# A decoder layer on one core: low parts on GpSimd in halves, output weights split sooner, key pages in groups of four

## The chip, the core and the metric

The kernel runs on one core of a Trainium2 chip. The metric is the device time of one execution in microseconds (us); the median of three runs of the kernel before is 780.32 us (780.12 to 782.49).

The core has a matrix engine (TensorE, "PE" in the profile; "PEld" is its loading of weights), a vector engine (VectorE, "DVE"), an activation engine (ScalarE, "ACT"), a general engine (GpSimd, "POOL") and a sync engine (SyncE, "SP") that issues all DMAs of this kernel. Each engine executes its instructions in the order of the program and waits where an operand is not ready.

## The reference

One decoder layer for a prompt of 1024 tokens and for 8 entries of 4 new tokens each (32 new tokens). One input projection feeds four heads of a gated linear recurrence (HGRN2) and eight heads of "forgetting" softmax attention (FoX); both are gated and go through one output projection.

```
q, k, v, log_f = ...                       # FoX: 8 heads of 64, from the input projection
c = cumsum(log_f)
s[t, s'] = q[t].k[s'] / 8 + c[t] - c[s']   # causal
o = softmax(s) @ v                         # prompt: blocks of 128 queries
# new tokens of entry j: keys and values are 2 cached pages of 128 rows
# (page_table[j]) and the entry's own new rows
x += concat(hgrn_out, o) * silu(gate) @ w_out
y = rmsnorm(x) * final_norm_w
```

All values are float32. To keep float32 accuracy with the faster matrix format, most operands are split into a high part (the value rounded to that format) and a low part (the value less its high part), and a product is made of hi x hi, hi x lo and lo x hi. The new tokens' products with the pages are made in plain float32, which is two passes for each matmul instruction of the program.

## The kernel before

**One stream beside a chain.** The main line writes out the recurrence of four heads and then attention, 32 steps: for each of four pairs of heads (`pr`), 8 steps of (head `i`, query quarter `q`). Beside it runs one stream of matmul work, `projections()` (L1357), a generator. Each `yield` of it hands back a price in planned microseconds; `fill(us)` in the main line takes steps from the stream until their prices have paid for `us`; if the next step waits for a flag, nothing is emitted and the rest of the `fill` is dropped. So the order of TensorE's instructions is set when the program is written out, by these prices. `defer(n, f)` emits `f` after `n` more steps of the stream.

**The stream.** Column slabs of the input projection (24 steps of 0.45 each), the values of a pair (`fox_values`, L776: they turn the value slab with transposes and split it), a pair's gate slab (`fox_gate`), then the output projection: `out_half` (L1234: four blocks of 128 tokens, for each half of the columns, with the first four of eight row blocks of the weights; four steps of 0.65), the new tokens (`fox_decode`, L1096), then `out_proj` for block 0, the new tokens (block 8), and blocks 1 to 7. `out_proj` of block 0 waits for flag "half0", that of block 8 for "A", that of block 3 for "half1", which is set behind the last attention step.

**A head's operands.** `fox_prep` (L839) makes, for one head, the high and low parts of Q and K (`Q1`, `K1`, `Q2`, `K2`) in four steps, which the main line takes one by one between its fills: two casts on DVE, two copies on ACT, the low part of Q on GpSimd (L854), the low part of K on DVE (L856). Attention of pair `pr` prepares pair `pr + 1` in its steps 5 and 7; the first pair is prepared in the main line ahead of attention (L1431 to 1437), with four fills of 0.77 a head.

**Attention steps.** `PLANS` (L983) gives the order in a step: "S" scores (two matmuls a tile, then DVE's mask and minimum), "E" exponential on ACT and normalisation on GpSimd (L910), "T" transposes (L925) and their split (ACT L929, DVE L930), "W" weighting of the values, "G" the output; numbers are fills, times 7.6, 6.4, 4.4 or 3.0 by the quarter, and for the last pair times 1.8.

**Output weights.** `wo_split` (L1037) makes high and low part of a block of the output weights, high on DVE, low on DVE or GpSimd. Those of the first half of the columns, blocks 0 to 2, are split at steps 12, 15 and 18 of the last gate slab. `m_split` (L1210) splits the gated outputs, high on ACT.

**New tokens.** `fox_decode` works on two groups of four entries. For each entry, four matmuls of its 32 queries (8 heads x 4 tokens, laid out by head pair) with 256 page columns, then four with the 32 new keys; each entry writes its own 32 partitions of one PSUM bank, so its weights take 32 of the array's 128 columns. `k_load` (L1071) brings an entry's pages, four entries at a time in four buffers. Then `soft` makes the softmax, and two groups of value products follow, with 512 columns. The first group of keys stands behind `out_half(2, 1)`, the rest behind the last `out_half`.

Of the kernel before, what the change touches and what calls it, by code (L numbers as in the profile page):

```python
# [19 lines left out]
T = 1024  # L20
# [4 lines left out]
ND = DB * DT  # L25
# [45 lines left out]
def tile_hymba(ctx, tc, x_prompt, x_sample, x_b, x_d, cache_k_t, cache_v, cache_logf_t, state_hgrn, page_table,  # L71
# [704 lines left out]
    def fox_values(pr):  # L776

        vf, pc = U(5), slice(pr * 128, (pr + 1) * 128)
        for g in range(2):
# [14 lines left out]
        p = ps_t()  # L794
        PE.transpose(p[:ND, :128], vf[:, T:], ident)
        A.activation(vdf[:, pc], p[:ND, :128], AF.Copy)
        defer(6, SP.dma_start, sv[:, pc], vdf[:, pc])
# [41 lines left out]
    def fox_prep(pr, i):  # L839
# [14 lines left out]
        G.tensor_sub(Q2[r], qf[r, :T], f32(Q1[r]))  # L854
        yield
        V.tensor_sub(K2[o], kf[r, :T], f32(K1[r]))  # L856
        flags.add(f"prep{pr}{i}")
        yield
# [178 lines left out]
    def wo_split(k, c):  # L1037
# [9 lines left out]
        (G if k % 2 and (k, c) != (3, 0) else V).tensor_sub(l, raw, f32(h))  # L1047
# [48 lines left out]
    def fox_decode():  # L1096
# [37 lines left out]
        for g in range(2):  # L1134
            if g:
                for j in range(4):
                    v_load(j)
                m_load(4, 0)
                m_load(5, 0)
            Sx.append(ps_pj()[:, :NK])  # L1140
            for j4 in range(4):
                j = 4 * g + j4
                kT = U(KT[j], 1024).rearrange("p (b a s) -> p a b s", b=2, a=4)
                for pr in range(4):
                    q = qb[:, pr, j].rearrange("p h t -> p (h t)")
                    mm(Sx[g][32 * j4:32 * j4 + 32, :PAST], q, kT[:, pr], pr == 0, pr == 3)
                    if pr == 1:
                        yield 0.9
                for pr in range(4):
                    q = qb[:, pr, j].rearrange("p h t -> p (h t)")  # L1150
                    mm(Sx[g][32 * j4:32 * j4 + 32, PAST:], q, kd[:, pr], pr == 0, pr == 3)
                k_load(j + 4)
                yield 1.0
            soft(g)
            yield 0.36
            if g == 0:
                yield None
# [76 lines left out]
    def out_half(tb, c):  # L1234
# [22 lines left out]
        if c == 0:  # L1257
# [4 lines left out]
            for j in ((0,), (1, 3), (2,), ())[tb]:  # L1262
                k_load(j)
# [93 lines left out]
    def projections():  # L1357
# [5 lines left out]
        for pr in range(4):  # L1363
            if pr < 3:
                yield from fox_gate(pr)
            else:
                for k in range(4):
                    wo_load(k)
                for i, us in enumerate(fox_gate(pr)):
                    if i in (12, 15, 18):  # L1370
                        wo_split(i // 3 - 4, 0)
# [12 lines left out]
        for c in range(2):  # L1384
            for tb in range(4):
                yield from out_half(tb, c)
                if c and tb == 2:
# [42 lines left out]
    flags.add("hgrn")  # L1430
    for i in range(2):  # L1431
# [3 lines left out]
        for _ in range(4):  # L1435
            prep_step()
            fill(0.77)
# [79 lines left out]
```

## Time and profile before

| | before |
|---|---|
| median of 3 runs | 780.32 us (780.12 to 782.49) |
| the profiled execution | 779.85 us |
| its span, first to last instruction | 778.1 us |
| TensorE busy | 740.7 us, 95% |
| DVE busy | 461.8 us, 59% |
| ACT busy | 356.9 us, 46% |
| GpSimd busy | 319.4 us, 41% |

The span is that of the profiled execution alone; 1.75 us of its time lie around it. A busy TensorE is not a TensorE at its peak, since matmuls are pipelined and their ends are modelled. The page's chain of waits follows back from the last instruction what released it. In a timeline each row has a start, a duration (neighbours of one kind merged, with their count), the engine, the line, the operation, output and inputs, and in brackets how long the engine sat idle before it and what ended that.

### The profile page before, as it was taken

The page shows a single profiled execution, that of the slowest core. Times are in us where ns is not written, and L with a number is a line of the kernel's source. Part 1 is how long each engine was busy: PE and PEld are TensorE (multiplying, and loading weights), DVE is VectorE, ACT ScalarE, POOL GpSimd, SP SyncE. Part 2 cuts the span into 40 slices and gives each one's busy share as a digit, 9 for nine tenths or more (in the row PEclk, how much of TensorE's full clock was granted, in tenths as well). Part 3 has the DMA queues.
Part 4 walks back from the last instruction along what each step waited for, and adds up shares of the span by engine and source line. Part 5 has one row for each costly group of instructions (what it writes and reads, how often), then busy time and mean ns, then how long its engine had stood idle before and what let it go on. Part 6 is the DMA issues. An engine that isn't in the chain of part 4 may idle for free.

```text
span 778.1 us, 12930 instructions
## 1 busy us (share of the span) xinstructions
PE 740.7 (95%) x4815; PEld 659.7 (85%) x4815; DVE 461.8 (59%) x954; ACT 356.9 (46%) x833; POOL 319.4 (41%) x337
## 2 busy tenths in 40 slices
PE   6999899999999999998999989989999899999996
PEld 5678899998999999997998889979988676577886
DVE  7774324646647665267447844785478776667422
ACT  4562446444242441136546654757466522455312
POOL 4450435373471853535434462536344533332101
PEclk8999999999999999999999999999999999999999
DMA  8411000100221103003101020101111686713521
GB/s 300 134 34 34 1 29 3 60 26 36 84 80 59 55 31 109 29 32 123 44 28 57 29 82 28 57 29 55 55 56 57 210 304 221 258 56 130 190 81 55
DMA packets 28465, 64.99 MB, mean 84 GB/s; under 512 B 6290, under 2 KB 7442, under 8 KB 28402
## 3 DMA queue, kind: packets, MB, share of 16 engines
q1 hardware_dynamic: 28402, 64.16, 23.6%
q8 instruction: 38, 0.62, 0.3%
q14 instruction: 25, 0.20, 0.1%
HBM read 47.27 MB, written 16.88 MB: 82 GB/s over the span
## 4 chain that ended last, share of the span: by engine, by line
PE 71%; DVE 15%; ACT 7%; issue 4%; POOL 1%; DMA 1%; SPq 0%; DVEq 0%; ACTq 0%; POOLq 0%
PE pj L95 52%; PE ps L95 11%; PE po L95 3%; DVE u L856 2%; PE pt L925 2%; DVE u L930 2%; DVE st L895 2%; PE pt L95 1%; ACT u L905 1%; ACT u L929 1%; DMA u<-in_w_dram 1%; DVE u L812 1%; ACT xhi L269 1%; POOL u L311 1%; DVE u L791 1%
## 5 line engine op out<-in xcount | busy, mean ns | idle before, releaser
L95 PE MATMUL pj<-xhi,u 128*128 128x352 f32 x1152 | 315.2, 332 | 0.7 <-DVE u L449 0.5
L95 PEld LDWEIGHTS pj<-xhi,u 128*128 128x128 f32 x1152 | 205.8, 188 | 3.4 <-DVE u L449 0.8
L95 PE MATMUL pj<-xlo,u 128*128 128x352 f32 x576 | 186.2, 323 | 0.0
L95 PE MATMUL ps<-u,u 128*128 128x64 f32 (+7 forms) x952 | 129.7, 272 | 3.4 <-ACT u L905 2.6
L95 PEld LDWEIGHTS ps<-u,u 128*128 128x128 f32 (+2 forms) x952 | 111.8, 178 | 14.4 <-ACT u L905 4.4
L910 POOL TENSOR_SCALAR u<-u,st 128x128 f32<-128x128 f32 (+3 forms) x64 | 48.7, 761 | 153.8 <-DVE st L908 87.7
L95 PEld LDWEIGHTS pj<-xlo,u 128*128 128x128 f32 x576 | 108.6, 189 | 0.7
L95 PE MATMUL pj<-u,xhi 128*128 128x260 f32 (+1 forms) x384 | 90.3, 329 | 4.1 <-DVE u L488 2.2
L905 ACT ACTIVATE u<-ps,st 128x512 f32<-128x512 f32 (+2 forms) x96 | 55.0, 578 | 50.3 <-DVE st L898 21.6
L95 PE MATMUL pj<-h,u 128*128 128x512 f32 (+2 forms) x237 | 74.3, 384 | 0.8 <-DVE h L1046 0.8
L655 POOL TENSOR_TENSOR u<-u,u 128x256 f32<-128x256 f32 (+1 forms) x56 | 40.4, 721 | 84.4 <-PE ps L95 78.8
L95 PEld LDWEIGHTS pj<-u,xhi 128*128 128x128 f32 x384 | 63.9, 191 | 12.2 <-ACT xhi L269 2.5
L930 DVE TENSOR_TENSOR u<-pt,u 128x512 fp32r<-128x512 f32 (+1 forms) x80 | 48.5, 631 | 29.3 <-ACT u L929 28.7
L95 PE MATMUL pj<-u,xlo 128*128 128x260 f32 (+1 forms) x192 | 62.6, 326 | 2.9 <-DVE xlo L273 2.9
L95 PE MATMUL po<-u,u 128*128 128x256 f32 (+1 forms) x320 | 52.3, 287 | 9.3 <-DVE u L930 4.7
L929 ACT ACTIVATE u<-pt 128x512 fp32r<-128x512 f32 (+1 forms) x80 | 41.8, 552 | 41.9 <-PE pt L925 34.2
L895 DVE TENSOR_REDUCE st<-ps 128x1 f32<-128x512 f32 (+2 forms) x96 | 53.3, 556 | 12.4 <-PE ps L95 9.8
L95 PEld LDWEIGHTS po<-u,u 128*128 128x128 f32 x320 | 44.3, 188 | 16.7 <-DVE u L930 7.8
L95 PEld LDWEIGHTS pj<-h,u 128*128 128x128 f32 (+1 forms) x237 | 42.3, 185 | 10.7 <-ACT u L811 1.2
L95 PE MATMUL pj<-u,u 128*128 128x512 f32 (+3 forms) x174 | 46.8, 437 | 2.7 <-ACT u L1213 2.1
L95 PE MATMUL pj<-w,u 128*128 128x512 f32 (+2 forms) x125 | 47.8, 383 | 0.0
L656 POOL TENSOR_TENSOR u<-u,u 128x256 f32<-128x256 f32 (+1 forms) x56 | 43.7, 780 | 0.0
(242 smaller groups left out, 1144.0 us busy)
## 6 DMA issues: line engine op xcount, KB each, us to landing
u<-in_w_s_dram SPq DMA_DIRECT2D x24, 512.0 KB
out_dram<-u SPq DMA_DIRECT2D x12, 512.0 KB
u<-in_x_b_dram SPq DMA_DIRECT2D x8, 512.0 KB
u<-in_cache_k_t_dram SPq DMA_DIRECT2D x16, 256.0 KB
u<-in_cache_v_dram SPq DMA_DIRECT2D x16, 256.0 KB
m_s<-u SPq DMA_DIRECT2D x7, 512.0 KB
u<-m_s SPq DMA_DIRECT2D x14, 256.0 KB
w<-in_w_out_dram SPq DMA_DIRECT2D x12, 256.0 KB
```

Source lines behind the costliest of these rows:

```text
L95: PE.matmul(out, lhsT, rhs, start=start, stop=stop, skip_group_check=True)
L269: A.activation(xhi[:, k, t0:t0 + n], xt[:, k], AF.Copy)
L311: se[a].tensor_sub(l[:, a], raw[:, a], f32(h[:, a]))
L655: G.tensor_mul(k4[:, :, 0, :], k4[:, :, 0, :], f3[:, eb, 1:2].to_broadcast([128, n, m]))
L656: G.tensor_mul(q4[:, :, 1, :], q4[:, :, 1, :], f3[:, eb, 0:1].to_broadcast([128, n, m]))
L856: V.tensor_sub(K2[o], kf[r, :T], f32(K1[r]))
L895: V.tensor_reduce(st[:, m:m + 1], ps, axis=AX.X, op=OP.min)
L905: A.activation(P[:, s], ps, AF.Exp, scale=-1.0, bias=st[:, lo:lo + 1], accum_out=st[:, 2 + m:3 + m])
L910: G.tensor_scalar(P[:, :e], P[:, :e], st[:, 4:5], 1.0, op0=OP.mult, op1=OP.mult)
L925: PE.transpose(p[:, c:c + 128], probs[n, b][:, j * 128:(j + 1) * 128], ident)
L929: A.activation(ph[:, :w], p[:, :w], AF.Copy)
L930: V.tensor_sub(pl[:, :w], p[:, :w], f32(ph[:, :w]))
```

## The change

Five edits. In `fox_values` the new tokens' part of the value slab is turned first, not last. In `fox_prep` both low parts are made on GpSimd, each in two halves of 512 columns, so that a preparation has six steps; the first pair's loop has six fills of 0.52, and the first pair's values are emitted ahead of it. `wo_split` of blocks 0 to 2 comes at steps 7, 10 and 13 of the last gate slab, and the low part of block 1 is made on DVE. The key pages of entry 1 are loaded with that of entry 0, and those of entries 2 and 3 one block later. In `fox_decode` the four entries of a group are worked on together, for one head pair after another, with prices of 0.45 a pair and 0.3 for the new keys in place of 1.9 an entry; pages of the next four entries are loaded together; and the first group stands behind `out_half(0, 1)`, two blocks sooner.

```diff
     def fox_values(pr):
         vf, pc = U(5), slice(pr * 128, (pr + 1) * 128)
+        p = ps_t()
+        PE.transpose(p[:ND, :128], vf[:, T:], ident)
+        A.activation(vdf[:, pc], p[:ND, :128], AF.Copy)
+        defer(6, SP.dma_start, sv[:, pc], vdf[:, pc])
         for g in range(2):
...
             yield 0.5
-        p = ps_t()
-        PE.transpose(p[:ND, :128], vf[:, T:], ident)
-        A.activation(vdf[:, pc], p[:ND, :128], AF.Copy)
-        defer(6, SP.dma_start, sv[:, pc], vdf[:, pc])
...
     def fox_prep(pr, i):
...
-        G.tensor_sub(Q2[r], qf[r, :T], f32(Q1[r]))
-        yield
-        V.tensor_sub(K2[o], kf[r, :T], f32(K1[r]))
-        flags.add(f"prep{pr}{i}")
-        yield
+        for x, X1, X2 in ((qf, Q1[r], Q2[r]), (kf, K1[r], K2[o])):
+            for c in range(2):
+                t = slice(512 * c, 512 * c + 512)
+                G.tensor_sub(X2[:, t], x[r, t], f32(X1[:, t]))
+                if x is kf and c:
+                    flags.add(f"prep{pr}{i}")
+                yield
...
     def wo_split(k, c):
...
-        (G if k % 2 and (k, c) != (3, 0) else V).tensor_sub(l, raw, f32(h))
+        (G if k % 2 and (c or k > 3) else V).tensor_sub(l, raw, f32(h))
...
     def fox_decode():
...
-            for j4 in range(4):
-                j = 4 * g + j4
-                kT = U(KT[j], 1024).rearrange("p (b a s) -> p a b s", b=2, a=4)
-                for pr in range(4):
-                    q = qb[:, pr, j].rearrange("p h t -> p (h t)")
-                    mm(Sx[g][32 * j4:32 * j4 + 32, :PAST], q, kT[:, pr], pr == 0, pr == 3)
-                    if pr == 1:
-                        yield 0.9
-                for pr in range(4):
-                    q = qb[:, pr, j].rearrange("p h t -> p (h t)")
-                    mm(Sx[g][32 * j4:32 * j4 + 32, PAST:], q, kd[:, pr], pr == 0, pr == 3)
-                k_load(j + 4)
-                yield 1.0
+            kTs = [U(KT[j], 1024).rearrange("p (b a s) -> p a b s", b=2, a=4) for j in range(4 * g, 4 * g + 4)]
+            qs = [[qb[:, pr, 4 * g + j4].rearrange("p h t -> p (h t)") for j4 in range(4)] for pr in range(4)]
+            for pr in range(4):
+                for j4 in range(4):
+                    mm(Sx[g][32 * j4:32 * j4 + 32, :PAST], qs[pr][j4], kTs[j4][:, pr], pr == 0, pr == 3)
+                if pr == 3:
+                    for j4 in range(4):
+                        k_load(4 * g + j4 + 4)
+                yield 0.45
+            for pr in range(4):
+                for j4 in range(4):
+                    mm(Sx[g][32 * j4:32 * j4 + 32, PAST:], qs[pr][j4], kd[:, pr], pr == 0, pr == 3)
+            yield 0.3
...
     def out_half(tb, c):
...
-            for j in ((0,), (1, 3), (2,), ())[tb]:
+            for j in ((0, 1), (2, 3), (), ())[tb]:
                 k_load(j)
...
     def projections():
...
-                    if i in (12, 15, 18):
-                        wo_split(i // 3 - 4, 0)
+                    if i in (7, 10, 13):
+                        wo_split(i // 3 - 2, 0)
...
-                if c and tb == 2:
+                if c and tb == 0:
                     for us in dec:
...
     flags.add("hgrn")
+    need("v0")
     for i in range(2):
         preps.append(fox_prep(0, i))
         fill(0.6)
         fox_const(i)
-        for _ in range(4):
+        for _ in range(6):
             prep_step()
-            fill(0.77)
+            fill(0.52)
```

## Rows read from the trace of the kernel before

**Rows 1.** The page, parts 1 and 4: busy times of engines, and the chain's shares.

```profile
PE 740.7 (95%) x4815; PEld 659.7 (85%) x4815; DVE 461.8 (59%) x954; ACT 356.9 (46%) x833; POOL 319.4 (41%) x337
PE 71%; DVE 15%; ACT 7%; issue 4%; POOL 1%; DMA 1%; SPq 0%; DVEq 0%; ACTq 0%; POOLq 0%
```

**Rows 2.** Busy times by stretch: length, PE, PEld, DVE, ACT, POOL, clock, DMA share, GB/s.

```profile
612.00:620.00 8.00, 4.56 (x15) 2.42 (x15) 6.12 (x8) 3.58 (x8) 4.35 (x5) 0.93 0.74 251
620.00:641.00 21.00, 21.00 (x99) 17.15 (x97) 14.21 (x31) 5.51 (x19) 7.11 (x8) 0.94 0.93 330
641.00:654.00 13.00, 13.00 (x88) 7.93 (x86) 7.03 (x19) 1.67 (x5) 4.42 (x4) 1.00 0.66 224
```

**Rows 3.** Timeline of PE, both groups of key products: first rows, and what follows each.

```profile
641.28 1.91 PE L95 MATMUL pj<-u,u 128*32 128x256 f32 x8
649.74 0.70 PE L95 MATMUL pt<-xd,cc 64*128 64x260 f32 x2
...
654.04 1.91 PE L95 MATMUL pj<-u,u 128*32 128x256 f32 x8
666.26 0.70 PE L95 MATMUL pt<-xd,cc 64*128 64x260 f32 x2
```

**Rows 4.** Timeline of PE, value products of the new tokens.

```profile
666.89 1.93 PE L95 MATMUL pj<-u,u 128*32 128x512 f32 x14
...
669.34 1.04 PE L95 MATMUL pj<-u,u 128*32 128x512 f32 x2
```

**Rows 5.** Timeline of PE in the tail: output projection, matmuls one behind the other.

```profile
743.58 0.63 PE L95 MATMUL pj<-h,u 128*128 128x512 f32 x2
...
744.27 0.63 PE L95 MATMUL pj<-h,u 128*128 128x512 f32 x2
```

**Rows 6.** Timelines of ACT and SP: the new tokens' queries, page loads, value loads.

```profile
633.39 1.95 ACT L1092 ACTIVATE u<-qd 64x32 f32<-64x32 f32 x8 [5.01 <-POOL u L1087]
...
644.40 6.04 SPq L1075 DMA_DIRECT2D u<-in_cache_k_t_dram  x8
656.33 4.01 SPq L1080 DMA_DIRECT2D u<-in_cache_v_dram  x8
```

**Rows 7.** Timelines of DVE and PE around the first output blocks.

```profile
612.10 1.50 DVE L1046 CAST u<-u 128x512 fp32r<-128x512 f32 x1 [1.40 <-POOL u L1047]
616.21 0.50 PE L95 MATMUL pj<-u,u 128*128 128x512 f32 x1 [2.11 <-ACT u L1213]
622.92 0.69 DVE L1256 TENSOR_TENSOR u<-u,pj 128x512 f32<-128x512 f32 x1 [3.27 <-DMA u<-in_x_prompt_dram]
624.00 0.86 PE L95 MATMUL pj<-u,u 128*128 128x512 f32 x3
```

**Rows 8.** By line (min/median/max ns), and POOL and DVE at one preparation.

```profile
L856 DVE TENSOR_TENSOR u<-u,u x8: 1221/3084/3391, 351.8 to 601.1; 64x1024 fp32r<-64x1024 f32 x8
L974 POOL TENSOR_TENSOR u<-u,u x15: 1259/1283/1297, 386.5 to 696.4; 64x512 f32<-64x512 f32 x15
...
601.00 2.39 POOL L854 TENSOR_TENSOR u<-u,u 64x1024 fp32r<-64x1024 f32 x1
601.09 3.39 DVE L856 TENSOR_TENSOR u<-u,u 64x1024 fp32r<-64x1024 f32 x1
```

**Rows 9.** Timeline of PE, idle time behind L856 in attention: the first.

```profile
428.44 0.36 PE L95 MATMUL po<-u,u 128*128 128x256 f32 x1 [1.08 <-DVE st L907]
```

**Rows 10.** Timelines of DVE, PE and POOL at the first pair's preparation.

```profile
356.74 1.26 DVE L791 CAST u<-u 128x256 fp32r<-128x256 f32 x3 [1.60 <-ACT u L785]
356.76 0.28 PE L795 MATMUL pt<-cc,u 128*32 128x128 f32 x1 [2.08 <-ACT u L785]
359.46 0.68 DVE L836 CAST u<-cc 64x1024 fp32r<-64x1024 f32 x1
365.68 0.82 POOL L910 TENSOR_SCALAR u<-u,st 128x128 f32<-128x128 f32 x2
366.10 0.89 PE L925 MATMUL pt<-cc,u 128*128 128x128 f32 x3
```

## The prediction

> **What bounds the kernel now.** I read the page first, then the chain of waits, then the busy times of chosen stretches, then the timelines of single engines. TensorE is busy 740.7 us of a span of 778.1 us, and PE holds 71% of the chain, DVE 15% [rows 1]. So an edit pays if it removes TensorE work, or ends a wait that TensorE sits in; the rest is free. Four stretches are touched.
>
> - 641 to 667 us, new tokens against the key pages: TensorE is busy the whole stretch, 13.00 us of 13.00 in its first half [rows 2].
> - 612 to 620 us, first output weights: busy only 4.56 us of 8.00, and the granted clock falls to 0.93 [rows 2].
> - The preparations of a head's operands inside attention (six, from 420 to 604 us): DVE's low part of K (L856) runs while GpSimd's low part of Q (L854) does.
> - The first pair's preparation, 347 to 372 us.
>
> What the filler does comes from the planner's own costs: each filler step carries a price, and each `fill` takes steps until its price is paid. I added these up by hand for both versions; where I say "steps", that is the source.
>
> **The change, part by part.**
>
> *Key pages in groups of four (the largest term).* Before, an entry sends eight passes of 128x256 and eight of 128x32 to one quarter of the array (32 columns), then the next entry does. The first eight take 1.91 us, and a group lasts from 641.28 to 649.74 and from 654.04 to 666.26 [rows 3]. Less what is interleaved (0.6 and about 4.1 us of attention) that is 7.8 + 8.1 = about 15.9 us. The value products show what the four quarters can do: fourteen passes of 128x512, for four entries, last 1.93 us, while two for one entry last 1.04 us [rows 4]. So passes for different quarters run side by side as long as the program has few in a row for the same one. The new order changes quarter after every two passes, as the value products do after every four. A group is then eight waves of 0.22 us (1.91 less one overhang, over eight) plus eight of 0.03: 2.0 us. Two groups: 4.0. Removed: 11.9 us of TensorE work.
>
> Where it lands: the planner's price of a group falls from 7.96 to 2.46, by 11.0 in all, so the same fills draw later steps forward: ten more steps of the output projection fall inside attention (it ends now with three steps of block 1 and the eight of block 2 still to do, afterwards with one of block 2). A step is three matmuls, 0.70 us (743.58 to 744.27) [rows 5]. So the tail after attention loses 10 x 0.70 = 7.0 us, and attention itself has 11.9 - 7.0 = 4.9 us less TensorE work.
>
> Not all of the 4.9 stays:
> - The first group now comes two blocks earlier, right behind the first second-half block, which ends near 634.8. Its queries are ready when ACT's eight copies from 633.39 end, 635.34 [rows 6]: about +0.6.
> - All four tiles must have landed before the first wave. The loads for entries 4 to 7 take SP 6.04 us of issue now, and the value loads 4.01 us from 656.33 [rows 6]; they now have only 12 projection steps (8.4 us) and a little attention to hide in, behind a queue that is full until 641 (DMA share 0.93, 330 GB/s) [rows 2]. Two MB at that pace is 6.3 us, so the last lands near 649 where TensorE wants it near 647.5: +1.5. The values then follow with about +1.
> - Twice the filler runs dry, waiting for the first half of the last head pair's output: 2.5 + 0.9 us of planned filler are missing. I take +1, since attention goes on meanwhile.
>
> Sum: -11.9 + 4.1 = -7.8; some changes of array layout fall away (about -0.7), so **-8.5**. Bounds: -13 (no wait) to 0 (every wait doubled and attention's own chain the bound).
>
> *First output weights.* GpSimd's second low part holds DVE's third cast (1.40 us idle before 612.10), DVE then holds ACT, and TensorE idles 2.11 us at 616.21 [rows 7]. All four raw tiles were loaded long before, so splits five steps earlier, with the second low part on DVE, end this. But what is late next is close: the first block's addition waits 3.27 us for the block of the input, which lands at 622.92 [rows 7], and the third block needs that PSUM bank back; TensorE reaches it at 624.00 now. With the input's load sitting behind two MB of weights, it does not come sooner. So **-0.4**; bounds -3 (if the input lands earlier) to 0.
>
> *Low parts on GpSimd, in attention.* L856 takes 3.39 us beside L854's 2.39 us, and 1221 ns at best [rows 8]: 3.39 is the rest of L854 and one L856 alone, so the two exclude each other. DVE loses it all; GpSimd gets four halves, each as L974 (64x512), 1283 ns: 5.1 us in place of 2.4. Behind the six L856 TensorE idles on a DVE releaser, first 1.08 us before 428.44 [rows 9]; there are eight such rows, of 0.30 to 1.72 us, 5.2 us in all. Now DVE is free there; GpSimd's normalisation (L910) can stand behind one half, at most 1.3 us, and has about half a step (some 5 us) to spare. Most of 5.2 goes: **-4.5**; bounds -7 and +1.
>
> *First pair: values ahead of the preparation.* TensorE's idle 2.08 us before the third transpose [rows 10] goes, as ACT's copies of the values are no longer behind the preparation's. But the preparation now waits for the values on DVE, which is in order. Values: 356.74 less 1.6 = 355.1, for 2.7 us (to 359.46 before) [rows 10]: 357.9. Then two constants and the cast of Q, 0.68 each: 359.9. From there GpSimd has nine instructions before its first L910: four halves of head 0, three of head 1, two low parts of the next gate weights (the same 512 columns), 9 x 1.28 = 11.5: 371.4, against 365.68 now [rows 10]. TensorE's first transposes (366.10) wait for L910. Late by 5.7; if five more DVE casts take turns with GpSimd, 5 x 0.68 = 3.4 more. In that time TensorE does two more gate steps (19 in place of 17), 2 x 0.48. So +4.7 to +8.1, or -2 if the chain is hidden after all; I take **+5.5**.
>
> The Trainium skill, "SBUF — State Buffer", section "Who interferes with whom", speaks against this part: a DVE instruction that needs the port pair shared with GpSimd is held until GpSimd's ends, and the other way round, for a whole instruction. By it the casts and halves run strictly one after the other and this part is +8.1; the 3.39 us of L856 agrees with it.
>
> *The new tokens' values first in every pair*, the page loads one block sooner: no cost seen; the former waits for the last chunk's evacuation, under 0.5 us a pair, inside the bounds above.
>
> **Sum.** -8.5 - 0.4 - 4.5 + 5.5 = -7.9. The profiled execution took 779.85 us (0.47 us below the median of the three runs, 780.32): 779.85 - 7.9 = **772.0 us**.
>
> **Rivals.**
> 1. *First pair hidden.* If GpSimd's chain is not what TensorE waits for, this part is -2: -8.5 - 0.4 - 4.5 - 2 = -15.4, 764.5 us. For: halves cover only 512 columns, and the first scores need few. Against: L910 is in order behind all of them.
> 2. *Loads decide.* Pages and values gate both groups; attention gains nothing and loses 5, so that part is -7.0 + 5 = -2: -2 - 0.4 - 4.5 + 5.5 = -1.4, 778.5 us. For: DMA share 0.93 until 641. Against: it falls to 0.66 after.
> 3. *The quarters don't overlap* (the change does not do what it says). The groups keep 15.9 us, the planner counts 4.9 for them; TensorE's sum is unchanged: 0 - 0.4 - 4.5 + 5.5 = +0.6, 780.5 us. For: each pass reads another tile. Against: the value products do too.
> 4. *GpSimd becomes the bound at every pair (slower).* Its work per preparation doubles, 2.4 to 5.1. If L910 ends last ahead of TensorE's transposes at each of the six preparations inside attention, each costs 1.3 (one half ahead of it), +7.8 in place of -4.5, and the first pair stands at its upper bound, +8.1: 7.8 + 8.1 - 8.5 - 0.4 = +7.0, 786.9 us. It decides once GpSimd's backlog exceeds the half step that L910 has to spare, some 5 us. For: GpSimd is late already in the first pair. Against: 319.4 us busy of 778.1 [rows 1].
>
> **How the numbers follow.** Forecast 0.50 (768 to 776 us), rival 1 0.23, rival 2 0.12, rival 3 0.06, rival 4 0.09. What a measurement can tell here is about 0.3%, 2.3 us. Faster: 0.50 + 0.23 + half of rival 2 = 0.79; within: 0.06 + 0.06 = 0.12; slower: 0.09. The range 762 to 780 leaves out rival 4, half of rival 3 and the far end of rival 1.
>
> **What would show it.** Right: a group of key products in about 2.0 us, four passes starting together; TensorE's last weighting some 4 us earlier relative to the gate's end and the stretch behind it 7 us shorter; no wait of DVE for GpSimd in the splits, but a wait of TensorE for DVE or DMA at the third output block; L856 gone and the idle behind it; in the first pair, transposes 5 us late with GpSimd as releaser. Wrong: key passes spaced 0.22 us one by one; L910 as releaser of L925 at later pairs; TensorE waiting several us for page or value loads.

## The result, and the profile after it

The changed kernel took 794.42 us (median of four runs, 791.61 to 795.91) beside 781.4 us of the kernel before on the same chip: ratio 1.0149, 95% interval 1.012 to 1.0177. It is slower by some 12 us; I had said 772.0, and 780 as the upper end; even the slowest rival that I wrote down stood at 786.9. The profiled execution took 791.61 us with a span of 789.6. Its page, parts 1, 2 and 4 (beside [rows 1]):

```profile
PE 740.5 (94%) x4815; PEld 663.2 (84%) x4815; DVE 445.5 (56%) x947; ACT 357.0 (45%) x833; POOL 342.8 (43%) x360
PEclk8999999999999999999999899999999989999999
PE 67%; DVE 11%; ACT 9%; issue 4%; POOL 4%; DMA 4%; SPq 0%; POOLq 0%; ACTq 0%; DVEq 0%
```

TensorE is busy as long as before, DVE 16 us less, GpSimd 23 us more, and the granted clock dips in two slices behind the first. To place the difference I took the start of each GpSimd normalisation (L910 before, L912 after; there is one for each block of 128 queries and head, numbered 0 to 63) as a milestone, and the lengths between milestones as a table, worked out from the traces (us; the first column from the second-last copy of the last HGRN head, L750, to normalisation 0; the last from normalisation 63 to the end of the span):

```
run                          first pair  0-14  14-17  17-47  47-51  51-54  54-63  tail
before                            19.52 63.14  14.03 149.15  22.93  22.09  63.94  77.14
after                             28.22 62.93  22.18 143.72  24.22  24.04  66.95  69.85
e1  first pair as before          19.70 62.17  14.71 144.95  23.00  22.66  71.73  69.52
e2  e1, all low parts as before   19.68 62.87  14.87 150.84  23.05  22.28  71.19  71.16
e3  e2, values order as before    19.54 63.15  14.04 149.13  22.21  22.30  71.58  71.14
e5  after, no wait for values     23.38 63.59  15.42 145.46  22.98  22.86  71.70  71.15
e6  after, first pair undivided   26.66 63.00  20.81 144.12  24.22  23.64  67.89  71.45
e12 e6, filler in phase           26.64 62.62  15.41 145.37  23.01  22.96  71.71  71.11
e8  e1, keys per entry            19.94 62.15  14.73 144.86  23.01  22.58  63.97  77.12
e7  e1, page loads sooner         19.95 62.15  14.71 144.92  23.00  22.40  71.99  69.92
e9  e7 at fill rate 1.55          19.68 62.15  14.91 144.89  23.00  19.62  66.29  76.83
e11 e8 at fill rate 1.55          19.68 62.16  14.91 144.87  23.01  19.66  67.50  88.08
x1  e1, no second loads           19.68 62.16  14.88 144.85  23.01  22.34  70.41  71.46
x2  e8, no second loads           19.68 62.15  14.73 144.92  23.01  22.33  63.99  77.06
```

Lines one and two of the table show where the time goes. The first pair is 8.7 us longer, the turn from the first to the second pair (14 to 17) 8.1 us longer, the body of attention 5.4 us shorter; behind it 1.3, 2.0 and 3.0 us are lost, and the tail gives 7.3 back. (The sum, 10.2, lacks 1.3 us of the 11.5 by which the spans differ: the changed execution was that much later already at the copy, and the other runs, with the same code up to there, are 0.1 to 3.4 us later than the kernel before.)

**The first pair** in the changed kernel. Timelines of DVE, POOL and PE (start, length, engine, line, out<-in, count, idle before and who ended it), which answer to [rows 10]:

```profile
348.76 0.69 DVE L750 COPY u<-pt 128x512 f32<-128x512 f32 x1 [0.60 <-PE pt L749]
356.85 1.26 DVE L795 CAST u<-u 128x256 fp32r<-128x256 f32 x3 [7.40 <-ACT u L789]
361.60 0.68 DVE L851 CAST u<-u 64x1024 fp32r<-64x1024 f32 x1
362.20 1.75 DVE L836 CAST u<-cc 64x1024 fp32r<-64x1024 f32 x1
363.87 1.74 DVE L837 CAST u<-cc 64x1024 fp32r<-64x1024 f32 x1
365.65 1.65 DVE L848 CAST u<-u 64x1024 fp32r<-64x1024 f32 x1
367.21 1.77 DVE L851 CAST u<-u 64x1024 fp32r<-64x1024 f32 x1
```

```profile
361.85 9.81 POOL L857 TENSOR_TENSOR u<-u,u 64x512 fp32r<-64x512 f32 x6 [3.14 <-DVE u L848]
371.74 1.29 POOL L449 TENSOR_TENSOR u<-u,u 128x512 fp32r<-128x512 f32 x1
...
375.71 1.64 POOL L912 TENSOR_SCALAR u<-u,st 128x128 f32<-128x128 f32 x3
```

```profile
362.98 0.30 PE L95 MATMUL ps<-u,u 128*128 128x128 f32 x1 [1.36 <-DMA u<-c_s]
...
366.80 0.48 PE L95 MATMUL ps<-u,u 128*128 128x128 f32 x1 [3.52 <-POOL u L857]
...
376.13 0.33 PE L927 MATMUL pt<-cc,u 128*128 128x128 f32 x1 [2.52 <-POOL u L912]
```

DVE stands idle for 7.40 us, from the copies of the last HGRN head to the first cast of the values; the preparation, which is queued behind the values, could have run there. When it runs at last, six halves (L857) take 9.81 us on GpSimd, and the casts beside them 1.65 to 1.77 us each in place of 0.68. TensorE waits 3.52 us for a half and 2.52 us for the first normalisation.

**The turn to the second pair**, busy times by stretch (length, PE, PEld, DVE, ACT, POOL, granted clock, DMA share, GB/s), then PE's two long waits:

```profile
362.00:376.00 14.00, 7.11 (x33) 6.71 (x33) 10.31 (x16) 7.97 (x18) 13.63 (x10) 0.88 0.21 80
436.00:440.00 4.00, 2.54 (x14) 2.07 (x15) 2.35 (x6) 3.16 (x9) 3.68 (x4) 0.80 0.14 52
440.00:444.00 4.00, 2.44 (x9) 1.89 (x9) 3.93 (x4) 1.19 (x2) 3.82 (x4) 0.77 0.27 92
444.00:448.00 4.00, 3.09 (x13) 3.09 (x14) 3.10 (x7) 0.00 (x0) 0.00 (x0) 0.65 0.00 0
```

```profile
438.19 0.95 PE L786 MATMUL pt<-cc,u 128*128 128x128 f32 x4 [1.41 <-ACT vdf L781]
...
444.91 1.61 PE L95 MATMUL po<-u,u 128*128 128x256 f32 x7 [2.47 <-DVE u L932]
```

```profile
441.42 1.37 DVE L795 CAST u<-u 128x256 fp32r<-128x256 f32 x1
442.83 1.43 DVE L796 TENSOR_TENSOR u<-u,u 128x256 fp32r<-128x256 f32 x1
```

The second pair's value transposes wait for ACT's copy of the new tokens' values, and a weighing waits for a split of DVE (L932) that stands behind value splits, which take 1.37 and 1.43 us beside GpSimd's halves and products (0.28 and 0.43 at 358.91 and 359.22 of the same trace). In the stretches with and behind these waits the granted clock is 0.77 and 0.65, that is, 46% and 70% of the stretch at 1.2 GHz and the rest at 2.4: here idle time is paid a second time as slow matmuls.

**Key pages.** Timeline of PE, both groups, which answers to [rows 3, 4], and of SP's queue:

```profile
649.19 1.93 PE L95 MATMUL pj<-u,u 128*32 128x256 f32 x32
650.94 0.56 PE L95 MATMUL pj<-kd,u 128*32 128x32 f32 x32
...
661.77 0.62 PE L95 MATMUL pj<-u,u 128*32 128x256 f32 x2
663.11 0.59 PE L95 MATMUL pj<-u,u 128*32 128x256 f32 x2 [0.72 <-DMA u<-in_cache_k_t_dram]
664.60 0.59 PE L95 MATMUL pj<-u,u 128*32 128x256 f32 x2 [0.90 <-DMA u<-in_cache_k_t_dram]
665.83 1.67 PE L95 MATMUL pj<-u,u 128*32 128x256 f32 x25 [0.64 <-DMA u<-in_cache_k_t_dram]
...
669.13 3.31 PE L95 MATMUL pj<-u,u 128*32 128x512 f32 x10
```

```profile
650.93 2.98 SPq L1281 DMA_DIRECT2D y_s<-u  x2
655.80 0.33 SPq L1235 DMA_DIRECT2D u<-in_x_prompt_dram  x1
656.39 4.16 SPq L1077 DMA_DIRECT2D u<-in_cache_k_t_dram  x8
```

The four quarters do run side by side: 32 passes in 1.93 us, the short ones in 0.56, a group in 2.2 us as I had worked out (2.0). The second group waits 0.72, 0.90 and 0.64 us for its pages, which SP issued from 656.39: ahead of them in its queue stood a load of the input (L1235) that was itself held until 655.80 by a spill of the same tile.

### The profile page after: what moved, and what is told of

Same layout as the page of the kernel before. It is cut to its first block, busy times and chain, and to the rows that moved or that the text cites. A ratio compares the mean times of both kernels' runs of the same rounds, so it can differ in the third digit from the quotient of the medians.

```text
span 789.6 us, 12946 instructions
## 1 busy us (share of the span) xinstructions
PE 740.5 (94%) x4815; PEld 663.2 (84%) x4815; DVE 445.5 (56%) x947; ACT 357.0 (45%) x833; POOL 342.8 (43%) x360
## 4 chain that ended last, share of the span: by engine, by line
PE 67%; DVE 11%; ACT 9%; issue 4%; POOL 4%; DMA 4%; SPq 0%; POOLq 0%; ACTq 0%; DVEq 0%
PE pj L95 48%; PE ps L95 11%; PE po L95 3%; PE pt L927 2%; POOL u L857 2%; DVE u L932 2%; DMA u<-in_cache_k_t_dram 1%; ACT u L907 1%; PE pt L95 1%; ACT u L931 1%; DVE u L796 1%; DVE u L795 1%; DMA u<-in_x_prompt_dram 1%; DMA u<-in_w_dram 1%; DVE st L897 1%
## 5 line engine op out<-in xcount | busy, mean ns | idle before, releaser
L95 PEld LDWEIGHTS pj<-xhi,u 128*128 128x128 f32 x1152 | 207.9, 190 | 3.5 <-DVE u L449 0.8
L912 POOL TENSOR_SCALAR u<-u,st 128x128 f32<-128x128 f32 (+3 forms) x64 | 48.2, 754 | 141.9 <-DVE st L910 93.7
L655 POOL TENSOR_TENSOR u<-u,u 128x256 f32<-128x256 f32 (+1 forms) x56 | 40.4, 721 | 84.4 <-PE ps L95 78.8
L932 DVE TENSOR_TENSOR u<-pt,u 128x512 fp32r<-128x512 f32 (+1 forms) x80 | 48.4, 632 | 34.4 <-ACT u L931 34.1
L927 PE MATMUL pt<-cc,u 128*128 128x128 f32 x288 | 43.7, 280 | 3.4 <-POOL u L912 3.4
L857 POOL TENSOR_TENSOR u<-u,u 64x512 fp32r<-64x512 f32 x32 | 44.1, 1388 | 4.7 <-DVE u L848 3.1
```

What stands on the lines that cost most here:

```text
L95: PE.matmul(out, lhsT, rhs, start=start, stop=stop, skip_group_check=True)
L655: G.tensor_mul(k4[:, :, 0, :], k4[:, :, 0, :], f3[:, eb, 1:2].to_broadcast([128, n, m]))
L857: G.tensor_sub(X2[:, t], x[r, t], f32(X1[:, t]))
L912: G.tensor_scalar(P[:, :e], P[:, :e], st[:, 4:5], 1.0, op0=OP.mult, op1=OP.mult)
L927: PE.transpose(p[:, c:c + 128], probs[n, b][:, j * 128:(j + 1) * 128], ident)
L932: V.tensor_sub(pl[:, :w], p[:, :w], f32(ph[:, :w]))
```

## The experiments

All ratios are to the kernel before, run beside the experiment on the same chip. e1 to e4, e5 to e8, e9 to e12, v1 to v3 and x1 to x3 each share the runs of the kernel before, and 1% is 7.8 us.

**Which part costs what: e1 to e3** take the change back, part after part. e1 has this edit, with the halves under an `else`; e2 drops the condition, so that the low parts are whole in all pairs; e3 has the four lines of the new tokens' values again behind the prompt's.

```diff
-    need("v0")
...
-        for _ in range(6):
+        for _ in range(4):
             prep_step()
-            fill(0.52)
+            fill(0.77)
...
+        if pr == 0:
+            G.tensor_sub(Q2[r], qf[r, :T], f32(Q1[r]))
+            yield
+            V.tensor_sub(K2[o], kf[r, :T], f32(K1[r]))
+            flags.add(f"prep{pr}{i}")
+            yield
```

e1: 

> The changed kernel with the first pair prepared as before: no wait for its values, four preparation steps, low parts of Q and K undivided (Q on GpSimd, K on DVE); everything later stays changed. Theory A (the loss starts in the first pair: its GpSimd halves and DVE casts hold each other, and the first normalisation is 10.0 us late): 794.4 - 10 = about 784 us, first normalisation near 365.7 us again. Rival B (that lateness is only moved: the filler taken there is missing later, so what is gained at 366 us is lost by the end of attention): 791 to 795 us, with the first normalisation early all the same.

e2: 

> The changed kernel with all low parts of Q and K as before (undivided, Q on GpSimd, K on DVE) and the first pair prepared as before; new tokens' values still first, weights and key pages still changed. Theory A2 (the further 6 us between the first and the second pair come from GpSimd halves beside DVE's value splits): 784 - 5 = about 779 us. Rival C (they come from the new tokens' value transposed first, which takes a PSUM bank that ACT empties late): no gain here, 783 to 785 us, and the gain comes in the next run. My prediction's term for the low parts (-4.5 us inside attention) would make this run 4.5 us slower than the one before it: 788 us.

e3: 

> As the run before, and the new tokens' values again behind the prompt's: what is left of the change is the first output weights and the key pages. Theory A2: as the run before, 779 us, some 2 us faster than the kernel before (781.4 here). Rival C: 783 or more before, 779 here, so 4 to 6 us faster than the run before. By my prediction's terms for these two parts alone (-8.5 and -0.4) it would be 772.5 us.

Measured: e1 777.86 us, 0.9941 (0.992 to 0.9962); e2 784.1, 1.0016 (0.9998 to 1.0034); e3 783.42, 1.0009 (0.9992 to 1.0026). e1 gained 2.1%, 16 us, more than theory A's 10: the turn to the second pair became normal with it (14.71 us). So what follows the first pair was the first pair's doing, not the halves beside the value splits: theory A2 failed, for e2 is slower than e1 by 0.75%, 5.9 us, all of it in the body (144.95 to 150.84). The halves on GpSimd gain inside attention what I had predicted. The order of the values (rival C) costs 1.7 us in the body at the most (e2 against e3), which the ratios can't tell from nothing. And e3, with nothing left but weights and key pages, is no faster than the kernel before, where I expected 772.5.

In e1 the preparation of the first head stands where DVE was idle before; DVE and POOL timelines:

```profile
348.55 1.73 DVE L836 CAST u<-cc 64x1024 fp32r<-64x1024 f32 x1
...
352.24 3.29 DVE L857 TENSOR_TENSOR u<-u,u 64x1024 fp32r<-64x1024 f32 x1
```

```profile
366.26 0.83 POOL L919 TENSOR_SCALAR u<-u,st 128x128 f32<-128x128 f32 x2
```

**The first pair taken apart: e5, e6, e12.** e5 is the changed kernel without the line `need("v0")`. e6 keeps it and has e1's undivided low parts for `pr == 0`. e12 is e6 with

```diff
     for i in range(2):
         preps.append(fox_prep(0, i))
-        fill(0.6)
+        fill(0.05)
```

e5: 

> The changed kernel without the wait for the first pair's values ahead of its preparation; the halves on GpSimd stay in all pairs. Run 1 showed that the first pair's preparation as a whole costs 2.1% (ratio to before 1.0149 with it, 0.9941 without), some 16 us. Theory A (its halves on GpSimd, each holding a DVE cast and held by one, are the loss): still 6 to 8 us late at the first normalisation, ratio 1.006 to 1.012. Rival F (the values ahead of it on DVE are the loss): first normalisation within 4 us of before, ratio 0.994 to 0.999.

e6: 

> The changed kernel with the wait for the values, but the first pair's low parts undivided (Q on GpSimd, K on DVE). Theory A: first normalisation 2 to 4 us late (the values' 3 us on DVE stand ahead), ratio 0.996 to 1.000. Rival F: 8 us or more late, ratio 1.008 to 1.014. If the further 6 us at the turn to the second pair (TensorE at a granted clock of 0.65 to 0.80 there) come from where the filler then stands, which the values' three early steps shift, they stay here: the turn shows an offset that grows by 5 us whatever the first normalisation does.

e12: 

> The run with the first pair's values ahead of an undivided preparation (ratio 1.0087), with 1.1 us of planned fill less in that preparation (0.05 in place of 0.6 ahead of each head's part), which is the price of the values' three steps taken early: the filler then stands at the same step when attention begins as in the kernel before. Theory J (the further 5 us at the turn to the second pair come from where the filler stands): the first normalisation stays about 9 us late, the jump at the turn goes, ratio 1.001 to 1.004. Rival K (the late first pair itself, with TensorE's clock down, makes the turn late): the jump stays, 1.007 to 1.010.

Measured: e5 783.1 us, 1.0007 (0.9987 to 1.0026); e6 789.9, 1.0087 (1.0056 to 1.0118); e12 785.77, 1.0026 (1.0006 to 1.0046). Against e1 the halves alone cost 0.66% (5 us), the wait alone 1.46% (11 us), both together 2.08%: they add up. Theory A missed both of its ranges; rival F's was met in e6 and just missed in e5. So the wait for the values is the larger cost, and the halves cost something too. The cost of the wait has two parts. In e6 the first pair is 7.1 us longer than in the kernel before, and the turn 6.8 us. e12 changes nothing but how much filler the first pair draws, 1.1 us by the planner's prices: the first pair stays as long (26.64), the turn is normal (15.41), and 0.61%, 4.8 us, come back. So the turn's loss is theory J's: the values' three steps (1.1 us by their prices) are drawn early, and the filler then stands two gate steps further on. Counted in the traces, 283 steps of the input projection lie ahead of attention's first transposes in the changed kernel and in e6, and 281 in the kernel before, e1, e5 and e12; between normalisations 14 and 17 it is 12 steps with the first two and 10 with the others. Rival K fell. Shown is that the place of the filler does it. That the next pair's value transposes and splits then collide with attention's own work is read from one trace only.

**The key pages: e4, e7, e8.** e7 is e1 with the edit below; e4 is e3 with 24 in place of 12; e8 is e1 with the key loop, its loads and its place (`tb == 2`) as before.

```diff
-            defer(6, x_load, tb, 1)
+            defer(12 if tb == 3 else 6, x_load, tb, 1)
```

e4: 

> As the run before, and the second half of the input's fourth block is loaded 24 filler steps after its first half's sum in place of 6, so that on SP's queue it no longer stands ahead of the key pages of entries 4 to 7 while it waits for the spill of the same tile. Theory D (what the key pages lost is this queue: in the changed kernel the pages are asked for at 656.4 us, 5.5 us after the spill ahead of them was asked for, and TensorE waits 2.3 us for them in three waits, some 3.5 us with the passes between): those waits go, 3 us less than the run before, 776 us. Rival E (the DMA queues are full anyway, and attention's own chain sets the end of this stretch): within 1 us of the run before.

e7: 

> The kernel of the first run (first pair as before, the rest of the change kept), with the second half of the input's fourth block loaded 12 filler steps after its first half's sum in place of 6: on SP's queue it then stands behind the key pages of entries 4 to 7, not ahead of them. Theory D (the pages wait in that queue behind a load that itself waits for a spill): TensorE's three waits for pages, 3.5 us in all, go; 3 us faster than that run, ratio 0.990. Rival E (attention's own chain ends that stretch, whatever the pages do): the waits go or shrink, the time stays, ratio 0.993 to 0.995.

e8: 

> The kernel of the first run with the new tokens' keys as in the kernel before: one entry after the other, one block earlier the loads and two blocks later the step as there. By my prediction's term (-8.5 for the key pages) this is 8.5 us slower than that run, ratio 1.005. Theory G (the 7.7 us of TensorE work saved are eaten by page waits and by waits of the last weighings of attention, as the traces of the runs so far show): within 1 us of it, ratio 0.993 to 0.996.

Measured: e4 785.9 us, 1.0037 (1.0016 to 1.0058), in which the load comes after the block's sum, so that the sum takes older data and the load waits for it; it tells nothing of the queue. e7 777.3, 0.9931 (0.9905 to 0.9956): the pages are now asked for at 637.36 and used at 644.12, the waits for them shrink to 0.28, 0.73 and 0.67 us, and the time does not move. Rival E holds. e8 778.4, 0.9939 (0.9918 to 0.996): with the keys entry by entry, as before, it is as fast as e1. The grouping, my largest term, is worth nothing that these intervals of some 2 us can see. (e8 takes the grouping, its loads and its place back together.) (The expectation's words on the loads of e8 mean that both stand where the kernel before has them.) The table shows the exchange: 54 to 63 is 7.8 us longer with the groups, the tail 7.6 us shorter.

**Fewer fills: e9 to e11.** e9 is e7, and e11 is e8, with the edit below; e10 is e7 with 1.65.

```diff
-    F3 = 1.8
+    F3 = 1.55
```

e9: 

> The kernel with the key pages' loads ahead of the input's load, and the last head pair's fills multiplied by 1.55 in place of 1.8. The sum of these fills is 77 us by the planner's prices at 1.8; the grouped key pages are priced 11.0 us less than before, so at 1.8 twelve more steps of the output projection were drawn into attention and the filler ran dry twice (1.3 and 0.9 us of fills unpaid). At 1.55 the same step as before is the next one when attention ends, and no fill is left unpaid. Theory H (the 8 us of TensorE work that the groups save are lost because the filler is still drawn at the old rate): attention ends some 8 us earlier, the tail is 8 us longer only against the run without the rate, ratio 0.987 to 0.990. Rival I (attention's own chain sets its pace whatever is drawn): what isn't drawn turns into waits, the tail is longer, ratio 0.995 to 1.003.

e10: 

> As the run before with 1.65: six steps fewer than at 1.8, no fill unpaid. Theory H: between the two, 0.988 to 0.991. Rival I: 0.993 to 0.998.

e11: 

> The control: the keys entry by entry as before (the run with ratio 0.9939) and the rate 1.55. Here the work inside attention shrinks by some 8 us and the tail grows by as much. If TensorE is what attention waits for at 1.8, the time stays, 0.993 to 0.996; if the rate is worth something by itself, it is below 0.991 here too, and a gain of the two runs above isn't the groups'; under rival I it is 0.998 or more.

Measured: e9 778.6 us, 0.9938 (0.9914 to 0.9963); e10 778.65, 0.9933 (0.991 to 0.9956); e11 789.24, 1.0077 (1.0052 to 1.0102). Theory H fell: against e7, e9's attention behind normalisation 51 is 8.5 us shorter and its tail 6.9 us longer, and the ratio does not move. The clearest readings are those of the stretch from normalisation 48 to 63. It takes 112.35 us in e7 and 103.87 in e9. e8, with nearly the tail of e9 and 11 us more of key work, takes 104.50. The control e11 has 36 matmuls of the output projection (twelve steps, 8.4 us by [rows 5]) fewer in the stretch than e8 and takes 105.12; its tail is 11 us longer. So work taken out shortens the stretch down to some 104 us, and no run here is below 103.87, though TensorE counts as busy in most of it. (Rival I's range is missed by 0.001 in e9 and met in e10 and e11.) Busy times from normalisation 48 to 63, e8 and e11:

```profile
594.88:699.38 104.50, 99.99 (x566) 70.24 (x567) 72.11 (x167) 44.21 (x113) 40.07 (x39) 1.00 0.58 195
593.00:698.12 105.12, 98.67 (x525) 67.48 (x526) 70.39 (x162) 41.14 (x105) 37.88 (x36) 0.97 0.56 184
```

With 41 matmuls fewer on record TensorE is busy for only 1.3 us less. A part of that is the clock: granted 1.00 in e8 and x2, 0.97 in e9, e11 and x3. At 0.97 some 6% of the stretch ran at 1.2 GHz, which by my estimate from these rows costs some 3 us. The 32 passes of the value products, 8.59 us in e8, take 13.20 in e11, the weighings 12.99 in place of 9.01 (from one matmul's start to the next, summed by form), with waits such as this one, PE's timeline of e11:

```profile
654.72 0.56 PE L95 MATMUL po<-u,u 128*128 128x256 f32 x3 [1.70 <-DVE u L939]
```

**Value products side by side: v1 to v3**, at the rates 1.8, 1.45 and 1.30: each half page for four entries in turn, priced 0.55; the second group's values are loaded into the key tiles, and three splits of merged blocks and a load move with it (not in the excerpt below). In these three the split of the seventh merged block is issued after the next load into its source tile, so it reads other data; the instructions are the same.

```diff
+            for b in range(2):
+                for j4 in range(4):
+                    vp = U(VT[4 * g + j4], 1024, a=2)
+                    mm(po[32 * j4:32 * j4 + 32], PT[g][:, b, 32 * j4:32 * j4 + 32], vp[:, b], b == 0, False)
...
+                yield 0.55
```

v1: 

> The run with the key pages' loads ahead of the input's load (0.9931), and the new tokens' value products of a group side by side too: for each half page the four entries in turn, priced 0.55 in place of 3.4, the second group's values loaded into the key tiles as soon as the keys are done with them. Theory L (the keys' gain was lost in value passes that come alone): the 32 value passes take 5 us in place of 11, and 3 us or more of that arrive in the time, ratio 0.987 to 0.990. Rival M (the filler now runs dry for 13 us of fills, and attention waits for its own results in that time, as in the runs before): ratio 0.992 to 0.997, with TensorE waiting behind the first key heads of the last pair.

v2: 

> As the run before, the last pair's fills multiplied by 1.45: one fill of 2.9 us unpaid. Theory L: 0.984 to 0.988. Rival M: what isn't drawn is waited for, 0.992 to 0.997.

v3: 

> As the run before at 1.30: no fill unpaid, and the same step as before comes next when attention ends, within one. Theory L (TensorE is what the last pair waits for, so 22 us less of planned work shorten it by most of what was saved): attention of the last pair 10 us shorter than in the kernel before, ratio 0.980 to 0.986. Rival M: 0.992 to 1.000.

Measured: v1 784.2 us, 1.0014 (0.9999 to 1.0029); v2 783.42, 1.0004 (0.9987 to 1.0021); v3 795.54, 1.0166 (1.0145 to 1.0187). Both theories missed their ranges: all three are slower than e7. The 32 value passes never came to the 5 us on which theory L builds: they take 13.38, 10.19 and 14.13 us, waits included, beside 11.08 in e7. So these runs do not test what passes side by side would be worth; they show that these versions don't get them. In v3 the value passes wait three times for their loads (2.01, 1.51 and 0.82 us), and one weighing waits 5.92 us for DVE.

**Without the second loads: x1 to x3.** x1 is e1, x2 is e8, and x3 is e1 at rate 1.55, each with

```diff
     def k_load(j):
-        if j < DB:
+        if j < 4:
...
-                    if g == 0 and b:
-                        v_load(j + 4)
```

x1: 

> The kernel of the first run (ratio 0.9941), leaving out the loads of the new tokens' pages for entries 4 to 7: their keys and values are taken from the tiles of entries 0 to 3, so the same passes run and 4 MB of loads are gone. Theory N (the loads decide: rival 2 of the prediction): with them gone, the 8 us that the groups save arrive, 6 us or more less than the first run, ratio 0.984 to 0.988, and 5 us or more less than the control beside it. Theory O (attention's own chain ends the stretch): 0.991 to 0.995, within 2 us of the control.

x2: 

> The control: the same loads left out with the keys entry by entry as before (0.9939 with the loads). TensorE never waited for them in that order, so both theories expect the same time as with them, 0.992 to 0.995; below 0.990, the loads cost this order something too, by what they hold on other queues.

x3: 

> The first of these three with the last pair's fills multiplied by 1.55, where no fill is left unpaid. Theory N: the gain arrives here as well or better, 0.980 to 0.988. Theory O: 0.992 or more, the steps not drawn turning into waits for attention's own results.

Measured: x1 777.67 us, 0.9932 (0.9905 to 0.9959); x2 777.77, 0.9932 (0.9909 to 0.9955); x3 778.25, 0.9943 (0.9923 to 0.9963). The control is as fast as the grouped order to 0.1 us, with 4 MB of loads gone: theory N fell for the second loads. x1's trace shows what stands there instead, PE's timeline, SP's queue and the stretch's busy times:

```profile
643.47 1.07 PE L95 MATMUL pj<-u,u 128*32 128x256 f32 x16
...
645.07 1.07 PE L95 MATMUL pj<-u,u 128*32 128x256 f32 x16
...
649.79 4.29 PE L95 MATMUL pj<-u,u 128*32 128x512 f32 x6 [2.70 <-DMA u<-in_cache_v_dram]
```

```profile
640.12 6.60 SPq L1286 DMA_DIRECT2D y_s<-u  x3
646.97 4.18 SPq L1089 DMA_DIRECT2D u<-in_cache_v_dram  x8
```

```profile
645.00:650.00 5.00, 2.30 (x53) 1.41 (x52) 4.72 (x15) 0.00 (x0) 3.17 (x3) 0.90 0.50 168
650.00:655.00 5.00, 5.00 (x8) 1.32 (x7) 0.40 (x1) 0.63 (x2) 0.05 (x1) 0.50 0.93 311
```

The keys take 4.5 us here, 16.0 in x2. But the value products then come 2.8 us after SP began to issue the first four entries' values, since the spills of the output projection's last sums hold its queue from 640.12 for 6.60 us. They wait 2.70 us, the granted clock of the five microseconds from 650 is 0.50 (all of it at 1.2 GHz), and six passes take 4.29 us. Before, 10.5 us lay between the issue at 656.33 and the first product at 666.89 [rows 4, 6], filled by the second key group [rows 3]. In this order the work that the change removes was the cover of the next loads.

The whole exchange, x2 to x1, from normalisation 52 to 63, in time from one matmul's start to the next: key passes -11.6; output projection +9.3 (twelve steps more); weighings +3.0; the wait ahead of the value products +2.8; value passes +2.3; scores +1.4; the rest -0.7: +6.4 in all (the terms are rounded). The tail, twelve steps or 8.4 us of matmuls shorter, is 5.6 us shorter in the table. Around normalisation 63 (703.64) the last weighings wait, here in x1:

```profile
701.64 0.39 PE L95 MATMUL po<-u,u 128*128 128x256 f32 x1 [0.63 <-ACT u L938]
...
703.17 0.58 PE L95 MATMUL po<-u,u 128*128 128x256 f32 x3 [1.15 <-DVE st L916]
...
713.50 0.62 PE L95 MATMUL po<-u,u 128*128 128x256 f32 x3 [0.93 <-DVE u L939]
```

Only the third of these waits lies in the tail (x2 has one of 0.31 there), with 0.33 us ahead of an output matmul. The granted clock is 0.86 from 700 to 705 and 0.80 from 705 to 710, beside 1.00 in x2, so the tail also starts with slow matmuls.

## Why the prediction was wrong

- **First pair, +5.5 forecast, +16 measured (after against e1).** The mechanism stood in the text, and my choice inside its bounds was too low: from the copy to the first normalisation it is 8.7 us longer, where I had 5.7, or 9.1 if DVE's casts take turns with GpSimd's halves (the +4.7 and +8.1 of the text have the two gate steps taken off). They do take turns. The step that failed is that I stopped there: "TensorE does two more gate steps (19 in place of 17)" was right, but I counted it as time won, and did not follow those steps to the next turn, where they cost another 5 to 7 us (14 to 17 in e6 and in the changed kernel, against e12). The Trainium skill, "SBUF — State Buffer", "Who interferes with whom", has GpSimd and a DVE instruction that needs the port pair shared with it exclude each other for a whole instruction. The trace agrees in kind: four casts and the halves take turns. By that rule one half and one cast take 1.28 + 0.61 = 1.9 us (the cast from 360.99 to the next at 361.60); in the trace the casts beside the halves follow each other at 1.67, 1.78 and 1.56 us (362.20, 363.87, 365.65, 367.21), so the exclusion is not quite whole, and the measurement decides.
- **Low parts in attention, -4.5 forecast.** Right: the body is 4.2 us shorter in e1 than before, and 5.9 us shorter than in e2. Rival 4, GpSimd as the bound at every pair, did not come.
- **First output weights, -0.4 forecast.** The size is about right: 47 to 51 is 0.7 us shorter in e3. TensorE's 2.11 us are gone; what is late next is not the third output block, as I had it, but 1.05 us on ACT, and 0.78 us on DVE as before. In e1 and e2, where the new tokens' values are first as well, 47 to 51 is 23.0 us and nothing is left of the gain. Timeline of PE, e3:

```profile
617.26 0.50 PE L95 MATMUL pj<-u,u 128*128 128x512 f32 x1 [1.05 <-ACT u L1214]
...
619.68 0.69 PE L95 MATMUL pj<-h,u 128*128 128x512 f32 x2 [0.78 <-DVE h L1046]
```

- **Key pages, -8.5 forecast, nothing measured (e1 against e8, x1 against x2).** The 11.9 us removed are right, to 0.3 (x1). Twelve steps were drawn into attention, not ten. The step that failed is "Not all of the 4.9 stays", where I put 4.1 us on what comes back. It is the whole 11.6, in x1 against x2: the wait for the values that I priced "about +1" is 2.8 us, with 2.3 us of slow passes after it; the weighings and the scores, which I gave no price, take 3.0 and 1.4 us more in attention, in idle time and slow passes; and the tail gives 2.8 us less than its twelve steps. Rival 2 (loads decide), at 0.12, was near in size. Of its cause the first values' wait is seen, but taking the second loads away did not bring the time back.
- **The new tokens' values first in every pair, "no cost seen".** Not settled: by the ratios of e2 and e3 nothing that can be told from zero; by their two traces 2.9 us in all, with 1.7 in the body, 0.8 each at the turn and from 47 to 51, and some gain elsewhere.

Summed by the runs: +16 - 5.9 and nothing for the rest is +10, the ratio's 12 less what the intervals leave open. What I read wrong at the start is [rows 2]: "busy 13.00 us of 13.00" does not say that a stretch ends when TensorE's work ends. e11 shows that it need not. What sets the 104 to 105 us of the last pair, if neither TensorE's work nor the second loads do, is open: the small waits of the weighings, the loads of the first values and the clock after each idle time show up together, and no run here separates them.

The best version is e1, or e7 with the same time: the change with the first pair's preparation as it was, 0.9941 (0.992 to 0.9962) and 0.9931 (0.9905 to 0.9956), 4.6 to 5.4 us faster than the kernel before.

## What to carry over

When a wait is put ahead of a queue, look at what the queue's engine would have done in that time: here DVE's 7.40 us of idle time were the price, and in e1, as before the change, they are work. When a planner fills by price, a few steps taken early move every later step, and the bill comes a whole pair later. And before work is removed from a busy engine, take other work out of the same stretch: if the stretch keeps its length, as in e11, the engine isn't its bound. Ask then what the work was the cover of; in x1 it was the next load.

## What was not expected of the hardware

- Thirty-two passes of 128x256, each into 32 columns, run in 1.93 us when the quarter changes after every two, where eight for one entry take 1.91 [rows 3]; a lone pair of 128x512 takes 1.02 to 1.05 us, ten passes in turn 1.92.
- The length of an idle time alone did not tell what the clock does. In the changed kernel the granted clock of the four microseconds behind TensorE's idle times of 3.52, 2.52, 1.41 and 2.47 us (to 366.80, 376.13, 438.19 and 444.91) was 0.57 to 0.60, and behind x1's 2.70 us it was 0.50 for five. But behind 1.91 us, to 459.44 of the changed kernel, and behind the 2.08 us before 356.76 in the kernel before [rows 10], it stayed 1.00.
- The kernel before varies from 779.81 to 785.59 us on one chip, with a mean granted clock of 0.992 to 0.983; the execution that I worked from, 779.85, is one of its fastest, so a stretch that it passes at full clock may be slower in others.
